# A searched order for a one-core decoder trunk: new orders for both plans, with the first output product inside the attention

## The chip, the cores and the metric

The kernel runs on one core of one Trainium2 chip. The metric is the device time of one execution in microseconds (us). Engines are named as in the profile: PE is TensorE (matmuls, with PEld for its weight loads), DVE is VectorE, ACT is ScalarE, POOL is GpSimd, SP is the engine that issues the transfers (DMAs).

## The reference

One layer over 1024 tokens of width 1024, everything in float32:

```python
h = rms_norm(x, norm1_g)
q, k, v, glu_a, glu_b = split(h @ w_in)            # five parts of 512 columns
q, k = rms_norm per head of 64 (8 heads)
attn = stick_breaking_attention(q, k, v)           # strictly causal, 128-query blocks
c = glu_a * sigmoid(glu_b)
c = silu(layer_norm(causal_depthwise_conv(c, 31 taps)))
x = x + concat([attn, c]) @ w_out
h = rms_norm(x, norm2_g)
gate, val = split(h @ w_up)                        # 2 x 2816 columns
gate = silu(causal_depthwise_conv(gate, 3 taps))
x = x + (gate * val) @ w_down
```

Stick-breaking attention weighs a key s before the query t by sigmoid(z) of its own score times the product of (1 - sigmoid(z)) of all keys between the two.

## The kernel before

**Products.** Every float32 operand is split into a high part (a rounded copy, made by ScalarE or by VectorE) and a low part (the difference, made by VectorE or GpSimd). `mm3` (L387 to L390) makes one product of three matmuls: high by high, high by low, low by high. A 128x512 output takes three matmuls for each 128 rows of the inner dimension.

**Stages.** (1) Input projection, GLU and 31-tap convolution, up to about 225 us. (2) Attention by head and half of the queries, up to about 414 us: `score` makes z, `below` (L1341) the sigmoids nb, `scan` (L1355) the running products, `turned` (L1374) transposes the weights into `wT`, `high` and `low` (L1385, L1395) split them, `products` (L1402) multiplies by v into the bank `po`, and `copied` and `summed` (L1430, L1436) put the head's rows into `attn`. Between these lie the convolution half of the output projection (`op`), whose sum with x is stored as `x_part`. (3) The attention half of the output projection by token tile of 128 (`opa`, in the order 0, 4, 1, 5, 2, 6, 3, 7), the second norm and the transposes `h2T` (L1678), from which the blocks 11, 21, 22, T1 to T4 are made: the operands of a seven-product (Strassen-like) scheme. (4) For each of 22 column blocks f of the FFN, seven products of 12 matmuls (11, 12, S2, S3, S1, S4, 22), sums into `gv`, and the activation. (5) The down projection (`dn`, L2099), from about 891 us.

**What sets the order.** Stages 1 to 4's beginning are written as two plans. Every piece of work is an operation made by `add(cost, emit, key, after, takes)`. Operations are numbered in the order in which they are defined. `ORDERS` holds one list of numbers for each plan, found by a search ahead of time; `plan.run` walks through the list, picks the engine where two are possible, gives out buffer slots and emits the instructions. `in_order` then chains the instructions of PE, DVE, ACT and POOL, each engine's in the order of the list. Transfers on SP are not chained, nor is the first plan with the second. Outside the plans the framework's scheduler places the instructions, and may move them between those of a plan.

**The first plan** ends with the last head (h = 7). The weights of the attention half of the output projection are loaded and split by `w_attn_rows` (L1547, L1551, L1556). **The second plan** begins with tile 0: its x is loaded back (L1623), the attention's rows of the tile are split into m (L1628 to L1638), two half products of 12 matmuls follow (`opa`, L388 to L390), and VectorE adds them to x (L1652). Its last part, `first_operands`, makes the operands and all seven products of FFN block 0, and the products 11 and 12 of block 1.

**Behind the second plan** stands the loop over f. For f = 0 the function `up` has no products left to make; it emits, in this order, y (ACT, L1948), two convolution steps (DVE, L1950), silu (ACT, L1952), the product with v (DVE, L1953) and a store. Then `sums_up(1)` emits the operands of block 1: three sums on POOL (L1769 to L1771), and for S2, S1, S3, S4 and 22 a cast on ACT (L384) and a subtraction on DVE (L385), with one more POOL sum (L1775) before S4. Products of block 1 other than 11 and 12 need those operands. The gate weights of block 2 are loaded into the buffer `raw0`, which holds those of block 1 until its operands are made.

Of the kernel before, what the change touches and what calls it, by code (L numbers as in the profile page):

```python
# [270 lines left out]
def kernel(  # L271
# [191 lines left out]
    def part_of(big_tile, i, words):  # L463
        return big_tile[:, i * words:(i + 1) * words]

    def in_order(start_at):
        last = {}
        for ins in nc.cur_bb.bb.instructions[start_at:]:
            if ins.engine in ORDERED:
# [1053 lines left out]
    for k in range(4):  # L1523
        w_out_rows(k)
# [615 lines left out]
```

## Time and profile before

| | |
|---|---|
| time, median of 3 runs | 1104.14 us (1103.88 to 1104.84) |
| the profiled execution's own time | 1106.51 us |
| its span | 1104.6 us |
| mean granted TensorE clock | 0.995 |
| matmuls, weight loads | 5258 each |
| DMA | 118.02 MB, mean 107 GB/s |

A row of a view by stretches gives, for each engine, its busy time in that stretch and in brackets the instructions that began there; PEclk is the clock that was granted to TensorE, as a share of full speed. A matmul of 128x512 is shown with some 0.39 us, but the next one starts 0.23 us after it: the matmuls overlap, so "busy" tells that TensorE had work, and the count of matmuls tells how much. A row of the waits gives the waiting instruction, what it waited for, the total, the times and the longest. A row of the timeline gives start, duration, engine, line, operation and tiles, and in square brackets the idle time ahead of it with what ended it.

### The profile page before, as it was taken

To read this page: it belongs to the slowest core of one execution; us is meant where nothing else is said; L and a number is where in the kernel's file an instruction comes from. 1 tells how busy PE (TensorE), PEld (TensorE's weight loads), DVE (VectorE), ACT (ScalarE), POOL (GpSimd) and SP (SyncE) were. 2 spreads that over 40 slices of the span, in tenths; PEclk is the share of its full clock that TensorE was granted. 3 is DMA by queue.
4 is the path that set the end of the run, shared out by engine and by line. 5 is a ranking of instruction groups with operands and counts; after the bars stand their busy time and mean duration, and the time that the engine had idled before them with its cause. 6 is when DMAs were issued, how large, how long until landed. Compare 5 with 4: busy or idle time off the path is not lost.

```text
span 1104.6 us, 14843 instructions
## 1 busy us (share of the span) xinstructions
PE 1091.2 (99%) x5258; PEld 908.6 (82%) x5258; DVE 882.3 (80%) x1201; ACT 586.5 (53%) x1044; POOL 591.0 (53%) x501
## 2 busy tenths in 40 slices
PE   8999999999999999999999999999999999999998
PEld 5888888888898887878888888888888888888887
DVE  6588998789999985889977777677777578797885
ACT  6354367576766663745333333343433388676760
POOL 4367889786722432894433223313322289887770
PEclk9999999999999999999999999999999999999999
DMA  8121210353843223523232222222231572403403
GB/s 271 39 58 39 86 49 20 86 177 105 260 119 95 96 91 139 188 80 96 96 107 65 96 77 82 90 77 96 71 102 58 175 301 77 152 22 132 153 5 149
DMA packets 110505, 118.02 MB, mean 107 GB/s; under 512 B 21369, under 2 KB 90208, under 8 KB 110430
## 3 DMA queue, kind: packets, MB, share of 16 engines
q1 hardware_dynamic: 110414, 117.06, 32.4%
q8 instruction: 42, 0.69, 0.3%
q14 instruction: 33, 0.27, 0.1%
q10 hardware_dynamic: 16, 0.00, 0.0%
HBM read 82.43 MB, written 28.31 MB: 100 GB/s over the span
## 4 chain that ended last, share of the span: by engine, by line
PE 96%; DVE 2%; ACT 1%; DMA 1%; issue 0%; SPq 0%; POOL 0%; DVEq 0%; POOLq 0%
PE dn L2099 19%; PE u_S L388 7%; PE u_S L389 7%; PE u_S L390 7%; PE u L390 5%; PE u L388 5%; PE u L389 5%; PE po L1402 3%; PE wT L1374 3%; PE qk L388 3%; PE qk L390 3%; PE qk L389 3%; PE z L1333 2%; PE z L1334 1%; PE opa L388 1%; PE opa L390 1%
## 5 line engine op out<-in xcount | busy, mean ns | idle before, releaser
L2099 PE MATMUL dn<-wd,wd 128*128 128x512 f32 x768 | 181.4, 389 | 0.0
L2099 PEld LDWEIGHTS dn<-wd,wd 128*128 128x128 f32 x768 | 144.2, 188 | 29.9
L388 PE MATMUL u_S<-bT,aS 128*128 128x512 f32 x264 | 102.7, 389 | 0.0
L389 PE MATMUL u_S<-bT,aS 128*128 128x512 f32 x264 | 102.7, 389 | 0.0
L390 PE MATMUL u_S<-bT,aS 128*128 128x512 f32 x264 | 102.6, 389 | 0.0
L2102 DVE TENSOR_TENSOR c<-dn,c 128x512 f32<-128x512 f32 x120 | 81.2, 686 | 24.9 <-PE dn L2099 24.6
L2004 ACT CAST wd<-rawd 128x512 fp32r<-128x512 f32 x128 | 72.8, 620 | 33.2 <-DMA rawd<-in_w_down_dram 10.0
L384 ACT CAST aS<-rawu 128x512 fp32r<-128x512 f32 x63 | 39.2, 624 | 94.6 <-PE u_S L390 66.1
L1355 DVE TENSOR_TENSOR_SCAN nb<-nb,one 128x384 f32<-128x384 f32 (+7 forms) x64 | 85.0, 1341 | 1.1 <-ACT nb L1341 0.9
L1769 POOL TENSOR_TENSOR s<-rawu 128x512 f32<-128x512 f32 x21 | 28.9, 1376 | 97.0 <-DMA rawu<-in_w_up_dram 95.6
L2003 ACT COPY whole<-rawd 128x512 f32<-128x512 f32 x110 | 63.5, 586 | 24.2 <-DVE wd L2005 11.4
L2005 DVE TENSOR_TENSOR wd<-whole,wd 128x512 fp32r<-128x512 f32 x90 | 59.9, 685 | 15.6 <-ACT wd L2004 8.5
L1775 POOL TENSOR_TENSOR rawu<-rawu 128x512 f32<-128x512 f32 x21 | 29.3, 1395 | 80.0 <-DVE a L385 79.9
L390 PE MATMUL u<-b,a 128*128 128x512 f32 x168 | 66.0, 393 | 2.0 <-DVE a L1903 2.0
L388 PE MATMUL u<-b,a 128*128 128x512 f32 x168 | 66.3, 394 | 0.0
L389 PE MATMUL u<-b,a 128*128 128x512 f32 x168 | 66.0, 393 | 0.0
L384 ACT CAST a<-rawu 128x512 fp32r<-128x512 f32 x61 | 37.9, 624 | 51.8 <-PE u_S L390 34.3
L1950 DVE SCALAR_TENSOR_TENSOR y<-gv,cols_a,y 128x1023 f32<-128x1023 f32 (+1 forms) x44 | 57.7, 1312 | 9.6 <-ACT y L1948 9.5
L1771 POOL TENSOR_TENSOR rawu<-s,rawu 128x512 f32<-128x512 f32 x21 | 31.7, 1508 | 49.6 <-DVE a L385 48.9
L389 PEld LDWEIGHTS u_S<-bT,aS 128*128 128x128 f32 x264 | 49.6, 188 | 10.3
L388 PEld LDWEIGHTS u_S<-bT,aS 128*128 128x128 f32 x264 | 49.6, 188 | 10.3
L390 PEld LDWEIGHTS u_S<-bT,aS 128*128 128x128 f32 x264 | 49.6, 188 | 10.3
(377 smaller groups left out, 3244.2 us busy)
## 6 DMA issues: line engine op xcount, KB each, us to landing
rawu<-in_w_up_dram SPq DMA_DIRECT2D x44, 512.0 KB
act_d<-y SPq DMA_DIRECT2D x22, 512.0 KB
rawd<-act_d SPq DMA_DIRECT2D x22, 512.0 KB
rawd<-in_w_down_dram SPq DMA_DIRECT2D x22, 512.0 KB
raw_qk<-in_w_in_dram SPq DMA_DIRECT2D x16, 256.0 KB
rawo<-in_w_out_dram SPq DMA_DIRECT2D x8, 512.0 KB
m<-conv_d SPq DMA_DIRECT2D x16, 256.0 KB
xt<-in_x_dram SPq DMA_DIRECT2D x8, 512.0 KB
```

The lines of the kernel that those rows point to most:

```text
L384: nc.scalar.copy(hi, src)
L388: nc.tensor.matmul(ps, a_hi, b_hi, start=first, stop=False)
L389: nc.tensor.matmul(ps, a_hi, b_lo, start=False, stop=False)
L390: nc.tensor.matmul(ps, a_lo, b_hi, start=False, stop=last)
L1355: nc.vector.tensor_tensor_scan(rev, rev, ones_of[0][:, :w], 0.0, op0=ALU.mult, op1=ALU.max)
L1374: nc.tensor.transpose(pt[:, 1 - j if diag else j, u * P:(u + 1) * P], ws[u][1]["nb"][:, ws[u][3] + sb * P:ws[u][3] + (sb + 1) * P], ident)
L1950: nc.vector.scalar_tensor_tensor(y[:, j:], g[:, :S - j], par("fw", (KF - 1 - j) * NF + f), y[:, j:], op0=ALU.mult, op1=ALU.add)
L2003: nc.scalar.copy(whole, src)
L2004: nc.scalar.copy(t[:, 0], src)
L2005: lo_engine.tensor_tensor(t[:, 1], whole, f32(t[:, 0]), op=ALU.subtract)
L2099: nc.tensor.matmul(ps, a[:, tok], b, start=first and m == 0, stop=last and m == 2, skip_group_check=True)
L2102: nc.vector.tensor_tensor(sums[c][s], ps, sums[c][s], op=ALU.add)
```

## The change

1. Both lists of `ORDERS` are replaced.
2. Costs in some operations are changed, and with them the engine that `plan.run` may pick. The normalising of x and the splitting of the `w_in` weights of v and qk are now marked `DVE2`, by which the planner reckons with DVE and POOL standing in each other's way.
3. The output product of tile 0 becomes 15 operations at the end of the first plan (`first_tile`), with m and x in the buffers raw0 and raw1 and its banks from those of the attention; the second plan has 8 operations fewer. The emitted instructions are the same in number and kind. Three dummy operations stand for the way from the last sums to the next tile.
4. The load of FFN block 0's first weights (into raw1) waits until tile 0's x has been used.
5. After the loop's first pass (f = 0) the instructions that it emitted on DVE, ACT and POOL are chained behind the second plan's last, in the order in which they were emitted. PE is left out of that chain.

By the new list the last operations of PE in the first plan are: `po` group 3 part 1, the first half product of tile 0 (1876 to 1879), `po` group 3 parts 2 and 3 (1720, 1724), the second half product (1881 to 1884). At the start, three transposes (tile 0's first half, both of tile 1) stand ahead of the first product of v; before it were tile 0's two. In the second plan PE's last eleven operations are 11 of block 0, two transposes of tile 7, 12 of block 0, 12 and 11 of block 1, and S3, S1, S2, 22, S4 of block 0.

```diff
 ORDERS = [[int(n) for n in numbers.split()] for numbers in ("""
...
+1870 1716 1876 1877 1722 1718 1723 1878 1879 1719 1720 1880 1724 1881 1882 1725
...
-    def in_order(start_at):
-        last = {}
+    def in_order(start_at, last=None, engines=ORDERED):
+        last = {} if last is None else last
         for ins in nc.cur_bb.bb.instructions[start_at:]:
-            if ins.engine in ORDERED:
+            if ins.engine in engines:
                 if ins.engine in last:
                     tc.add_manual_dep(ins, last[ins.engine].name, mybir.DependencyInfo(
                         mybir.DependencyClass.NoSync, mybir.DependencyReason.DATA), reason="planned order")
                 last[ins.engine] = ins
+        return last
...
-            c = add({"DVE": 560, "ACT": 650}, lambda eng, i=i, cols=cols: (
+            c = add({"DVE2": 520, "ACT": 830}, lambda eng, i=i, cols=cols: (
...
-            a = add({"ACT": 1330, "DVE": 1120}, high, T(at_ - LEAD_W), [x, begun_at], d["rooms"])
+            a = add({"ACT": 1440, "DVE2": 960}, high, T(at_ - LEAD_W), [x, begun_at], d["rooms"])
...
+    def first_tile(t, key):
+        d = tile_0
...
+        xl = add("SP", 4000, load, key - 2, [stored[t]], [xr])
+        a = add("ACT", 250, m_high, key, halves_done[0], [mr])
+        b = [add({"DVE2": 260, "POOL": 460}, low(3, lambda: attn[1][:, tok]), key, [a])]
+        a = add("ACT", 480, lambda: nc.scalar.copy(d["m"][:, 0, :3], attn[0][:, :, tok]), key, [a])
+        b += [add({"DVE2": 560, "POOL": 1000}, low(slice(0, 3), lambda: attn[0][:, :, tok]), key, [a])]
+        adds = []
+        for nn in range(2):
...
+                m = add("PE", 681, products, key + 0.1, b + last_unit + ([m] if m else []), [] if kk else [o])
+            f = add("DVE", 690, lambda nn=nn, cols=cols: nc.vector.tensor_tensor(d["x"][:, cols], d["ps", nn], d["x"][:, cols], op=ALU.add), key + 0.1, [m, xl])
...
+    first_tile(TOKENS[0], base - 0.4)
+    waits = add("DVE", 560, lambda: None, base, [add("ACT", 480, lambda: None, base, [halves_done[1][-1]])])
+    add("PE", 20, lambda: None, base + 0.5, [waits])
 
     plan.run(ORDERS[0])
     in_order(start_at)
...
-        a = add("ACT", 250, m_high, mk, [], [mr])
+        a = add("ACT", 250, m_high, mk, [last_sums] if t > 3 else [], [mr])
...
-        x1 = add("SP", 4500, lambda: load(0), key - 3)
+        x1 = add("SP", 4500, lambda: load(0), key - 3, tile_0["room"].users)
...
     plan.run(ORDERS[1])
-    in_order(start_at)
+    last_planned = in_order(start_at)
+    start_at = len(nc.cur_bb.bb.instructions)
...
         if f + 1 < NF:
             A = sums_up(f + 1, raw_next)
+        if f == 0:
+            in_order(start_at, last_planned, ORDERED[1:])
```

More of the change, by code (lines that the diff above doesn't have):

```diff
@@ L514, in load_x @@
         op = add("SP", 3500, load, key)
-        if not t:
-            op.moves = [Plan.HALF] * 2
+        if t < 2:
+            op.moves = [(360, 1500, 1750)] if t else [Plan.HALF] * 2
         return op
@@ L533, in roots @@
             nc.gpsimd.tensor_tensor(d["rs"], d["rs"], expo[:, :1], op=ALU.pow)
-        a = add("ACT", 1070 if t else 800, square, T(at_), [x], [r])
+        a = add("ACT", 1250 if t else 820, square, T(at_), [x], [r])
         b = add("POOL", 950, roots, T(at_), [a])
@@ L618, in weights @@
         x = add("SP", 3500, load, T(at_ - LEAD_LOAD) if key is None else key, [], [room])
-        x.moves = [Plan.PIECE] * 2 if len(srcs) > 1 else [Plan.COLUMNS]
+        x.moves = [(430, 2200, 1250 if name == "v_0" else 800), Plan.PIECE] if len(srcs) > 1 else [Plan.COLUMNS]
         if shape[0] < ND:
-            a = add({"ACT": 1330, "DVE": 1120}, high, T(at_ - LEAD_W), [x, begun_at], d["rooms"])
+            a = add({"ACT": 1440, "DVE2": 960}, high, T(at_ - LEAD_W), [x, begun_at], d["rooms"])
             b = add({"DVE2": 1480, "POOL": 3700}, low, T(at_ - LEAD_W + 0.5), [a])
@@ L1270, in unit @@
         return kst, k_ready, vst, v2
+    halves_done = [[], []]
     for h, half in [(h, half) for h in range(H) for half in range(2)]:
@@ L1440 @@
                 po.users += [a, b]
+                halves_done[half].append(b)
             prev_last = last
@@ L1519, in conv_half @@
                 xr.users += [f]
-            st = add("SP", 4000, lambda t=t, d=d: nc.sync.dma_start(x_part[t], d["x"]), k(1.2), sums)
+            st = stored[t] = add("SP", 4000, lambda t=t, d=d: nc.sync.dma_start(x_part[t], d["x"]), k(1.2), sums)
             xr.users += [st]
+    stored = {}
     for k in range(4):
@@ L1568, with load, m_high, low @@
     prev_last.after += last_unit
+    tile_0 = {}
+    def first_tile(t, key):
+        d = tile_0
+        tok = slice(t * P, (t + 1) * P)
+        mr, xr = [plan.token("wt", free=True) for _ in range(2)]
+        mr.only, xr.only = (0,), (1,)
+        def load():
+            d["x"] = raw([P, D], F32, f"x2_{t}", 1)
+            nc.sync.dma_start(d["x"], x_part[t])
+        def m_high():
+            d["m"] = raw([P, 2, 4, P], F32R, f"m{t}", 0)
+            nc.scalar.copy(d["m"][:, 0, 3], attn[1][:, tok])
+        def low(part, src):
+            return lambda eng: (nc.vector if eng == "DVE" else nc.gpsimd).tensor_tensor(d["m"][:, 1, part], src(), f32(d["m"][:, 0, part]), op=ALU.subtract)
+        xl = add("SP", 4000, load, key - 2, [stored[t]], [xr])
[5 more added lines that the diff above has]
+        for nn in range(2):
+            o, m = plan.token("o"), None
+            cols = slice(nn * 512, (nn + 1) * 512)
+            for kk in range(4):
+                def products(nn=nn, kk=kk, cols=cols, o=o):
+                    if kk == 0:
+                        d["ps", nn] = bank(o, [P, 512], f"opa{t}_{nn}")
+                    mm3(d["ps", nn], d["m"][:, 0, kk, :], d["m"][:, 1, kk, :], w_attn[ROWS[kk]][0][:, cols], w_attn[ROWS[kk]][1][:, cols], kk == 0, kk == 3)
+                m = add("PE", 681, products, key + 0.1, b + last_unit + ([m] if m else []), [] if kk else [o])
+            f = add("DVE", 690, lambda nn=nn, cols=cols: nc.vector.tensor_tensor(d["x"][:, cols], d["ps", nn], d["x"][:, cols], op=ALU.add), key + 0.1, [m, xl])
+            mr.users += [m]
+            o.users += [f]
+            adds.append(f)
+        mr.users += b
+        xr.users += adds
+    first_tile(TOKENS[0], base - 0.4)
+    waits = add("DVE", 560, lambda: None, base, [add("ACT", 480, lambda: None, base, [halves_done[1][-1]])])
+    add("PE", 20, lambda: None, base + 0.5, [waits])
     plan.run(ORDERS[0])
@@ L1612, with opa @@
     raws, block_done = {}, {}
-    def tokens(t, key):
-        hr, r = [plan.token(name) for name in ("h2", "small")]
-        xr, mr = plan.token("xt"), plan.token("m")
-        d = {}
-        tok = slice(t * P, (t + 1) * P)
-        where = (slice(None), slice(None), slice(t % 4 * P, (t % 4 + 1) * P))
+    def opa(t, key, d, tok, xr, adds):
+        mr = plan.token("m")
+        if t == TOKENS[1]:
+            mr.only = (1,)
         def load():
@@ L1631, in tokens @@
         xl.moves = [(360, 1500, 1800)]
-        adds = []
         mk = key + M_AT
-        a = add("ACT", 250, m_high, mk, [], [mr])
+        a = add("ACT", 250, m_high, mk, [last_sums] if t > 3 else [], [mr])
         b = [add({"DVE2": 260, "POOL": 460}, lambda eng: (nc.vector if eng == "DVE" else nc.gpsimd).tensor_tensor(
@@ L1655, in tokens @@
             adds.append(f)
+    def tokens(t, key):
+        hr, r = [plan.token(name) for name in ("h2", "small")]
+        d = {}
+        tok = slice(t * P, (t + 1) * P)
+        where = (slice(None), slice(None), slice(t % 4 * P, (t % 4 + 1) * P))
+        if t == TOKENS[0]:
+            d.update(tile_0)
+            xr, adds = Plan.Token("raw"), [add("DVE", 10, lambda: None, key, [attention_ends])]
+            tile_0["room"] = xr
+        else:
+            xr, adds = plan.token("xt"), []
+            opa(t, key, d, tok, xr, adds)
         st = add("SP", 3000, lambda: nc.sync.dma_start(x2_d[t], d["x"]), key, adds)
```

161 rows, old and new, of the table ORDERS are left out of this document.

## The prediction

> **What bounds the kernel now.** I read the page's busy times first, then stretches of the span side by side, then the waits of TensorE.
>
> ```profile
> span 1104.6 us, 14843 instructions
> PE 1091.2 (99%) x5258; PEld 908.6 (82%) x5258; DVE 882.3 (80%) x1201; ACT 586.5 (53%) x1044; POOL 591.0 (53%) x501
> ```
> ```profile
> core 0: us, PE busy (x) PEld busy (x) DVE busy (x) ACT busy (x) POOL busy (x), PEclk, DMA share, GB/s
> 7.00:14.00 7.00, 3.32 (x20) 2.12 (x19) 5.09 (x6) 6.04 (x11) 4.75 (x5) 1.00 1.06 377
> 14.00:19.00 5.00, 5.00 (x15) 3.93 (x16) 5.00 (x9) 3.84 (x7) 1.98 (x4) 0.66 1.04 403
> 50.00:225.00 175.00, 175.00 (x795) 144.39 (x794) 147.45 (x213) 93.93 (x180) 135.03 (x125) 1.00 0.20 58
> 225.00:406.00 181.00, 180.38 (x1177) 159.28 (x1176) 167.49 (x221) 124.67 (x248) 91.01 (x79) 1.00 0.43 129
> 406.00:415.00 9.00, 7.00 (x52) 6.00 (x51) 7.74 (x12) 6.71 (x13) 4.29 (x4) 0.99 0.79 255
> 415.00:419.00 4.00, 3.97 (x11) 3.11 (x12) 1.19 (x3) 0.39 (x1) 0.09 (x1) 0.61 0.56 221
> 466.00:479.20 13.20, 10.98 (x55) 8.47 (x53) 13.06 (x16) 9.90 (x19) 11.89 (x11) 1.00 0.39 121
> 479.20:483.00 3.80, 3.71 (x9) 2.95 (x10) 3.80 (x8) 1.74 (x3) 2.46 (x3) 0.55 0.15 45
> 483.00:500.00 17.00, 17.00 (x76) 13.96 (x75) 13.94 (x15) 6.64 (x11) 16.52 (x11) 1.00 0.29 83
> 500.00:1080.00 580.00, 580.00 (x2561) 480.41 (x2560) 447.72 (x602) 287.95 (x468) 281.10 (x209) 1.00 0.30 102
> ```
> ```profile
> PE v L739 <- DVE hi_v L598: 3.7, 2, 1.9
> PE u L390 <- DVE a L1903: 2.0, 1, 2.0
> PE opa L388 <- ACT m L1637: 1.4, 1, 1.4
> ```
> TensorE is the bound: 99% busy. From 500 to 1080 us it starts 2561 matmuls in 580 us, 0.2265 us for each 128x512 product, with no gap. So only four places can give anything. Each of the three great waits (DVE hi_v, ACT m, DVE a) is followed by a stretch with a granted clock of 0.66, 0.61 or 0.55, where busy TensorE starts fewer matmuls than the time has room for. A wait here is paid twice: as idle time and as slow clock.
>
> **The change part by part.** No instruction is added to or taken from any engine; the dummy operations of the new plan emit nothing. All is order.
>
> (a) *Tile 0's output product.* Counting the operations of the first plan in their order of definition, 1876 to 1879 and 1881 to 1884 are the two half products (12 matmuls each). The new list puts the first half ahead of the last head's last two `po` groups (1720, 1724) and the second half behind them.
>
> ```profile
> 412.53 0.38 PE L1402 MATMUL po<-tl,rest 128*128 128x256 f32 x1 [0.34 <-DVE tl L1395]
> 412.99 0.63 PE L1402 MATMUL po<-diagonal,rest 128*128 128x256 f32 x4
> 413.66 0.58 ACT L1430 COPY attn<-po 64x512 f32<-64x512 f32 x1 [0.96 <-PE po L1402]
> 414.27 0.89 DVE L1436 SCALAR_TENSOR_TENSOR attn<-po,v_ends,attn 64x256 f32<-64x256 f32 x2 [0.26 <-ACT attn L1430]
> 414.47 0.93 ACT L1637 CAST m<-attn 128x384 fp32r<-128x384 f32 x2
> 415.03 0.80 PE L388 MATMUL opa<-hio,m 128*128 128x512 f32 x1 [1.41 <-ACT m L1637]
> ```
> Lost here now: 9.00 - 7.00 = 2.0 us idle, and behind it 4.00 - 11 x 0.2265 = 1.5 us of slow clock; 3.5 in all. What is late next is tile 4, the first that needs the attention's end: copy 0.58, sums 0.89, half of the 0.93 cast, and three hand-overs of about 0.04, some 2.1 us behind the last `po`. The second half product takes 12 x 0.2265 = 2.7 us and covers it; without it the 1.4 us wait is back. The first half covers the wait on `tl`. Tile 0's load of x and its casts are moved past each other and past two weight loads on SP; they are 0.3 to 0.5 us pieces on engines with room (ACT 6.71 of 9 us). Value -3.5. Bounds: -3.5, and +1 if the last row of `w_out` is late and the product waits instead.
>
> (b) *The end of the second plan.* Lost now: 13.20 - 10.98 = 2.2 us idle and 3.80 - 9 x 0.2265 - 0.1 = 1.7 us of clock; 3.9.
>
> ```profile
> 475.79 1.77 DVE L1825 TENSOR_TENSOR a<-rawu,a 128x512 fp32r<-128x512 f32 x1
> 477.09 1.60 POOL L1832 TENSOR_TENSOR rawu<-rawu 128x512 f32<-128x512 f32 x1
> 477.49 1.75 DVE L1903 TENSOR_TENSOR a<-rawu,a 128x512 fp32r<-128x512 f32 x1
> 511.74 0.68 DVE L385 TENSOR_TENSOR aS<-rawu,aS 128x512 fp32r<-128x512 f32 x1
> ```
> VectorE is busy 13.06 of 13.20 us, and the same subtraction that takes 0.68 with GpSimd idle takes 1.75 beside a GpSimd tensor operation. The new order moves subtractions of tiles 4 and 5 (operations 49, 54, 56 and 111 of the old count) further ahead, into the time when both engines have room, so fewer collide at the end. A shift of the whole stage by (a) alone would leave this wait as it is, for the engines' inputs come at TensorE's pace. Bounds -3.9 and +2 (one more such collision of 1.1 us, and its clock). I take -3.3, nearest to the full removal, since 2 us of wait need only two of the 1.1 us collisions gone.
>
> (c) *The start.* Lost now: 7.00 - 3.32 = 3.7 us and 5.00 - 15 x 0.2265 = 1.6 us; 5.3.
>
> ```profile
> 9.54 0.80 PE L739 MATMUL v<-hi_v,h_hi 128*128 128x512 f32 x2 [1.82 <-DVE hi_v L598]
> 13.87 0.96 PE L739 MATMUL v<-hi_v,h_hi 128*128 128x512 f32 x3 [1.86 <-DVE hi_v L598]
> 10.37 3.44 DVE L598 TENSOR_SCALAR hi_v<-raw_v,gain 128x512 fp32r<-128x512 f32 x2
> 11.12 2.41 POOL L608 TENSOR_TENSOR lo_v<-raw_v,hi_v 128x1024 fp32r<-128x1024 f32 x1
> ```
> The second pair of `hi_v` took 3.44 us where the first two took 0.88, beside GpSimd's 2.41. The new order splits the second tile's work ahead of it and puts three turns of x in front of the first product: the second wait goes, the first grows, as tile 1 is normalised only after 10 us. Bounds -3.7 (first wait and half of the clock) and +1.5; I take -1.5, since TensorE is then in steady flow about 1 us sooner and part of the slow clock goes.
>
> (d) *The rest of the first plan.* From 50 to 225 us TensorE has no idle time, from 225 to 406 us 181.00 - 180.38 = 0.6, and small waits hidden in modelled ends. Bounds -2 and +2; I take -0.8.
>
> (e) *The wait that is added.* After the first FFN column block the change chains VectorE, ScalarE and GpSimd in the order of the code. There `up(0)` (the depthwise convolution, silu and product of block 0) stands ahead of `sums_up(1)` (the operands of block 1). In the trace they ran the other way:
>
> ```profile
> 488.93 0.62 ACT L384 CAST aS<-rawu 128x512 fp32r<-128x512 f32 x1 [2.77 <-POOL rawu L1770]
> 498.37 0.68 DVE L1868 TENSOR_TENSOR gv<-u_S,gv 128x512 f32<-128x512 f32 x1
> 499.08 1.25 ACT L1948 ACTIVATE y<-gv,cols_a 128x1024 f32<-128x1024 f32 x1 [0.53 <-DVE gv L1868]
> 500.36 2.60 DVE L1950 SCALAR_TENSOR_TENSOR y<-gv,cols_a,y 128x1023 f32<-128x1023 f32 x2 [0.21 <-ACT y L1948]
> 505.54 1.28 ACT L1952 ACT_TABLE_LOAD   x1
> 506.84 1.07 ACT L1952 ACTIVATE y<-y 128x1024 f32<-128x1024 f32 x1
> 510.10 1.72 DVE L1953 TENSOR_TENSOR y<-gv,y 128x1024 f32<-128x1024 f32 x1
> ```
> The cast at 488.93 for block 1 ran 10 us ahead of block 0's y. Chained, it queues behind y and silu on ScalarE, and its subtraction behind two convolution steps and the product on VectorE. TensorE is who waits: y needs block 0's last product (S4), block 1's products 11 and 12 are already used up, all others need these operands, and block 2's first weights go into the slot that block 1's operands are made from. From the last matmul of S4: its 0.39 us end, sum 0.68, y 1.25, steps 2.60, silu 1.07, product some 1.3 (1.72 beside GpSimd), subtraction 0.68, hand-overs 0.15: 8.1 us to the first matmul with a low part, less three slots of 0.2265: 7.4 us. A slow clock follows, as behind each wait above (1.5 to 1.7): 1.4. Bounds: 0, if the operands still come in time, and 12 with the 1.28 table load in the path and two slow stretches; nothing of it can be a gain, for TensorE has no gap from 483 to 500. I take +8.8.
>
> Sum: -3.5 - 3.3 - 1.5 - 0.8 + 8.8 = -0.3 us. It is made against the profiled span of 1104.6 (that execution's own time is 1106.51, 1.9 more); the median of the runs shown, 1104.14, is 2.4 below that execution, and I carry the difference over: **1103.8 us**.
>
> [...]
>
> **The rivals.** 0.2% (2.2 us) is about what a measurement of this kernel can tell from no change.
> - *The chain costs nothing*: the operands of block 1 are made in cover. For it: that chain concerns 18 instructions only; against it: the second plan's chain, made in the same way, was kept on VectorE where a later instruction was ready:
>
> ```profile
> 483.47 0.59 ACT L1875 COPY gv<-u 128x512 f32<-128x512 f32 x1 [1.86 <-PE u L390]
> 489.00 0.69 DVE L1868 TENSOR_TENSOR gv<-u_S,gv 128x512 f32<-128x512 f32 x1 [1.25 <-PE u_S L390]
> 489.61 0.68 DVE L1868 TENSOR_TENSOR gv<-u,gv 128x512 f32<-128x512 f32 x1
> ```
> The sum at 489.61 had its inputs at 484.1, and VectorE sat idle 1.25 us for the one ahead of it. Sum -9.1: 1095.0. Chance 0.15.
> - *The order gives more*: the start gives 4.5, the second plan's end 3.9, the middle 1.5. For it: all of that is idle time in the rows above; against it: the first product cannot start before `hi_v`, at 9.54. -3.5 - 3.9 - 4.5 - 1.5 + 8.8 = -4.6: 1099.5. Chance 0.25.
> - *Slower: VectorE stays the bound at the second plan's end.* The wait at 477 us is not recovered, since VectorE there has 0.14 us of room in 13.2: -0.3 + 3.3 = +3.0: 1107.1. It decides from 2.5 of the 3.3 us lost again; with the table load in (e)'s path 1108.4. Chance 0.22.
> - *Short waits cost no clock*: then (a) gives 2.0, (b) 1.7, (c) 1.1, (d) 0.8, and (e) stays at 8.8: +3.2, 1107.3. The clocks of 0.61 and 0.55 behind the two waits speak against it. Chance 0.02. [...]
>
> **How the numbers follow.** The forecast (no change that can be told) has 0.36, and 1102 to 1106.3 as its own range. Faster by over 0.2%: 0.15 + 0.25 = 0.40; slower: 0.22 + 0.02 = 0.24. Two cases of opposite sign (the price of the chain and the gains of the order) nearly cancel, so the range must hold both rivals: 1095 (chain free) to 1109 (its table load in the path, VectorE still the bound), with less than 2 in 10 outside.
>
> **What would show each step.** (a) no wait of `opa` on ACT `m`, and clock 1.00 in the 5 us behind the attention; (b) no wait of `u` on DVE `a`; (c) one wait on `hi_v` in place of two; (e) a wait of 6 to 8 us of `u_S` on a VectorE or ScalarE instruction of `sums_up(1)`, about 15 us behind the second plan's last `h2T`, with y at L1948's place ahead of all casts of block 1, and a slow clock behind it. The prediction is wrong if (e) shows no gap (then about 1095), or if a new wait stands between 50 and 406 us, where I saw hardly any room.

## The result

The changed kernel takes **1115.52 us** (median; 1114.90 to 1116.06) against 1104.49 us before (the three runs of the table of before and one more): ratio 1.0099, 95% interval 1.0081 to 1.0116. It is 11 us slower. The forecast was 1103.8 us, with a range that ended at 1109.

The page of the changed kernel begins so (its profiled execution took 1115.21 us, span 1112.9):

```profile
span 1112.9 us, 14818 instructions
PE 1088.1 (98%) x5258; PEld 905.4 (81%) x5258; DVE 871.7 (78%) x1200; ACT 586.9 (53%) x1050; POOL 580.6 (52%) x496
```

The work is the same: 5258 matmuls, and 2746 instructions on VectorE, ScalarE and GpSimd together in both. But ScalarE runs 6 more, VectorE 1 and GpSimd 5 fewer: by the new costs some changed their engine, so the change is not order alone, though the prediction says so. The span is 8.3 us longer. Where, is read from equal stretches of both spans. Before:

```profile
core 0: us, PE busy (x) PEld busy (x) DVE busy (x) ACT busy (x) POOL busy (x), PEclk, DMA share, GB/s
0.00:25.00 25.00, 20.19 (x81) 13.12 (x82) 14.15 (x28) 16.67 (x31) 10.21 (x22) 0.93 0.88 298
25.00:400.00 375.00, 374.38 (x2068) 319.38 (x2067) 325.66 (x448) 228.33 (x446) 232.65 (x209) 1.00 0.31 92
400.00:425.00 25.00, 22.97 (x123) 19.18 (x121) 17.50 (x24) 12.50 (x23) 8.95 (x8) 0.93 0.43 147
...
475.00:525.00 50.00, 48.02 (x204) 38.94 (x203) 45.67 (x49) 24.11 (x38) 32.46 (x23) 0.97 0.26 78
525.00:1080.00 555.00, 555.00 (x2450) 459.69 (x2450) 423.99 (x577) 275.33 (x449) 271.66 (x203) 1.00 0.30 102
```

After:

```profile
0.00:25.00 25.00, 21.43 (x94) 13.74 (x94) 14.21 (x31) 18.99 (x35) 6.83 (x21) 1.00 0.88 298
25.00:400.00 375.00, 370.27 (x2046) 315.74 (x2047) 314.40 (x438) 227.23 (x445) 236.81 (x211) 1.00 0.31 93
400.00:425.00 25.00, 22.99 (x129) 19.29 (x128) 19.87 (x28) 12.24 (x25) 7.09 (x7) 1.00 0.36 128
...
475.00:525.00 50.00, 39.57 (x166) 31.72 (x166) 38.69 (x45) 20.20 (x32) 26.28 (x18) 0.90 0.22 64
525.00:1080.00 555.00, 555.00 (x2450) 459.73 (x2449) 425.98 (x577) 276.78 (x453) 272.48 (x203) 1.00 0.30 102
```

Read the count of matmuls behind "PE busy". From 475 to 525 us all have the same shape: 166 in place of 204, and 38 x 0.2265 = 8.6 us. From 525 us on both kernels run 2450 in 555 us; nothing differs. At the start and at the attention's end the count is higher and the clock is 1.00 in place of 0.93, but in the middle (25 to 400 us) PE has 4.7 us without work where it had 0.6.

In the sections below "lost" is this: for each two neighbouring matmuls the time from start to start, less the step that undisturbed matmuls of those shapes take (0.2265 us for 128x512), added up over a stretch of the trace. It holds idle time and slow clock together. How the undisturbed step is chosen moves the row from 25 to 400 us by several us, but in all columns alike: the differences between the columns move by some 0.3 us.

| stretch, us | before | after | after without the chain |
|---|---|---|---|
| 0 to 25 | 9.45 | 7.89 | 8.01 |
| 25 to 400 | 16.55 | 19.33 | 19.34 |
| 400 to 425 | 5.07 | 3.49 | 3.44 |
| 425 to 475 | 2.06 | 1.73 | 1.64 |
| 475 to 525 | 4.29 | 12.83 | 1.69 |

TensorE's waits, after (what waited, for what, total us, times, longest):

```profile
PE u_S L387 <- ACT aS L383: 10.4, 1, 10.4
PE v L739 <- DVE lo_v L604: 1.9, 1, 1.9
PE qT L1290 <- DVE diagonal L1391: 1.7, 1, 1.7
...
PE wT L1375 <- DVE tl L1396: 1.2, 1, 1.2
PE glu_a L387 <- ACT cpad L827: 1.1, 1, 1.1
...
PE opa L387 <- ACT m L1683: 0.8, 1, 0.8
```

Of the three great waits of before, those on `hi_v` and on `a` are gone and that on `m` is 0.8 us in place of 1.4. In their place stand one of 10.4 us and a handful of 1 to 2 us. The long one in order of time (start, duration, engine, line, what, and in brackets the idle time before it with its releaser):

```profile
492.51 0.39 PE L389 MATMUL u_S<-b,aS 128*128 128x512 f32 x1
...
492.81 1.26 POOL L1829 TENSOR_TENSOR s<-rawu 128x512 f32<-128x512 f32 x1 [1.30 <-DMA rawu<-in_w_up_dram]
...
494.10 0.62 ACT L383 CAST aS<-s 128x512 fp32r<-128x512 f32 x1 [9.96 <-POOL s L1829]
494.75 1.08 DVE L384 TENSOR_TENSOR aS<-s,aS 128x512 fp32r<-128x512 f32 x1 [4.51 <-ACT aS L383]
495.76 0.68 DVE L1928 TENSOR_TENSOR gv<-u_S,gv 128x512 f32<-128x512 f32 x1
...
496.47 1.24 ACT L2009 ACTIVATE y<-gv,cols_a 128x1024 f32<-128x1024 f32 x1 [1.75 <-DVE gv L1928]
497.74 2.60 DVE L2011 SCALAR_TENSOR_TENSOR y<-gv,cols_a,y 128x1023 f32<-128x1023 f32 x2 [0.71 <-ACT y L2009]
500.42 1.28 ACT L2013 ACT_TABLE_LOAD   x1 [2.71 <-DVE y L2011]
501.72 1.06 ACT L2013 ACTIVATE y<-y 128x1024 f32<-128x1024 f32 x1
...
502.68 0.60 ACT L383 CAST aS<-rawu 128x512 fp32r<-128x512 f32 x1
...
503.33 0.79 PE L387 MATMUL u_S<-bT,aS 128*128 128x512 f32 x1 [10.43 <-ACT aS L383]
```

The reader is to see two things. From 495.76 on it is the forecast's path: last sum, y, two steps, silu, then the first cast of block 1, one after another on two engines. But the last sum's input was ready at 492.9, and it starts 2.9 us later, because VectorE holds another instruction: the subtraction at 494.75. It needs the cast at 494.10, and that the sum `s` at 492.81, for which GpSimd had waited for a transfer (`rawu`). Block 1's own `s` had been made at 487.46, so this is an operand of block **2**. Number 4 below, which holds back block 2's operands, takes it away.

### The profile page after: what moved, and what is told of

Read it like the earlier page. It is cut to its first block, busy times and chain, and to the rows that moved or that the text cites. A ratio compares the mean times of both kernels' runs of the same rounds, so it can differ in the third digit from the quotient of the medians.

```text
span 1112.9 us, 14818 instructions
## 1 busy us (share of the span) xinstructions
PE 1088.1 (98%) x5258; PEld 905.4 (81%) x5258; DVE 871.7 (78%) x1200; ACT 586.9 (53%) x1050; POOL 580.6 (52%) x496
## 4 chain that ended last, share of the span: by engine, by line
PE 86%; POOL 4%; DVE 3%; DMA 3%; ACT 2%; issue 2%; SPq 0%; DVEq 0%; POOLq 0%; ACTq 0%
PE dn L2162 19%; PE u_S L387 7%; PE u_S L388 7%; PE u_S L389 7%; PE u L387 5%; PE u L389 5%; PE u L388 5%; PE po L1403 3%; PE wT L1375 3%; PE qk L387 3%; PE qk L389 3%; PE qk L388 3%; POOL attn L879 2%; PE z L1334 2%; PE z L1335 1%
## 5 line engine op out<-in xcount | busy, mean ns | idle before, releaser
L387 PE MATMUL u_S<-bT,aS 128*128 128x512 f32 x264 | 103.9, 393 | 10.4 <-ACT aS L383 10.4
L1356 DVE TENSOR_TENSOR_SCAN nb<-nb,one 128x128 f32<-128x128 f32 (+7 forms) x64 | 84.6, 1340 | 0.6 <-ACT nb L1342 0.5
L2011 DVE SCALAR_TENSOR_TENSOR y<-gv,cols_a,y 128x1023 f32<-128x1023 f32 (+1 forms) x44 | 58.3, 1326 | 10.5 <-ACT y L2009 10.4
L389 PEld LDWEIGHTS u_S<-bT,aS 128*128 128x128 f32 x264 | 49.7, 188 | 10.4
L384 DVE TENSOR_TENSOR a<-rawu,a 128x512 fp32r<-128x512 f32 x61 | 45.4, 746 | 16.0 <-ACT a L383 16.0
```

Of the source, the lines that this page charges most:

```text
L384: lo_engine.tensor_tensor(lo, src, f32(hi), op=ALU.subtract)
L387: nc.tensor.matmul(ps, a_hi, b_hi, start=first, stop=False)
L389: nc.tensor.matmul(ps, a_lo, b_hi, start=False, stop=last)
L1356: nc.vector.tensor_tensor_scan(rev, rev, ones_of[0][:, :w], 0.0, op0=ALU.mult, op1=ALU.max)
L2011: nc.vector.scalar_tensor_tensor(y[:, j:], g[:, :S - j], par("fw", (KF - 1 - j) * NF + f), y[:, j:], op0=ALU.mult, op1=ALU.add)
```

## The experiments

Every kernel but the second starts from the changed one. Times are medians; the kernel before took 1104.92, 1105.07 and 1104.36 us beside the three sets.

**1. The chain left out** (both new orders stay).

```
         if f + 1 < NF:
             A = sums_up(f + 1, raw_next)
-        if f == 0:
-            in_order(start_at, last_planned, ORDERED[1:])
```

> The changed kernel without the chain behind the first FFN column block; both new orders stay. Theory (the chain carries the loss): the 10.4 us wait of u_S on aS and the slow clock behind it (2.3 us above the 0.2265 us step) are gone, nothing else moves: 1115.5 - 12.7 = 1102.8 us, so within 2 us of the kernel before, and the cast of block 1's S1 is ahead of y on ScalarE again. Rival 1 (the new orders lose time of their own, behind 475 us too): a wait of 3 us or more stays at 480 to 510 us and the time is 1106 or more. Rival 2 (the stall comes from the weights' transfers, and the chain only lies beside it): 1113 or more.

Measured 1103.13 us (1102.25 to 1103.84), ratio to before 0.9986, interval 0.9977 to 0.9995. The chain costs 12.4 us (by the lost time from 475 to 525 us of the two traces 11.1); all else together gains 1.8 (by the interval 0.6 to 2.5). The waits that remain:

```profile
PE hT L556 <- DVE x_k L549: 3.1, 2, 2.7
PE qT L1290 <- DVE diagonal L1391: 1.7, 1, 1.7
...
PE glu_a L387 <- ACT cpad L827: 1.2, 1, 1.2
...
PE opa L387 <- ACT m L1683: 0.8, 1, 0.8
PE u_S L389 <- DVE aS L1885: 0.7, 1, 0.7
```

No wait for an operand of block 1 is left (L1885 is block 0's own); behind the start the others stand as they did with the chain.

**2. The chain alone, on the kernel before** (both orders old; the same two lines and the argument of `in_order` added there).

> The kernel before with the chain alone; both orders are the old ones. Theory (the chain stalls TensorE whatever the order): one wait of 9.5 to 11 us of u_S on aS behind the second plan, about 2 us of slow clock, 1104.5 + 12 = 1116.5 us. Rival 1 (the chain hurts only in the new second order): a wait below 5 us, 1108 or less. Rival 2 (the forecast's size, 7.4 us of wait and 1.4 of clock): 1113.3.

Measured 1116.11 us, ratio 1.0109 (1.0095 to 1.0122). The chain does not need the new orders to do its harm. The wait itself was 7.6 us, not 9.5 to 11 as I expected: here the subtraction of block 2 was through (495.45 us) before block 0's last sum was due (496.88).

```profile
PE u_S L388 <- ACT aS L384: 7.6, 1, 7.6
```

TensorE lost 14.9 us from 475 to 525 us in place of 4.3. Of the 10.6 us more, 7.6 are the wait; the other 3.0 fit the slow clock behind it (21 products in 7.6 us at a granted clock of 0.63, which is 2.8 us more than they need).

**3. The chain kept, block 1's operands written ahead of `up(0)`.**

```
+        if f == 0:
+            A_1 = sums_up(1, raw_next)
         up(f, A)
         if f + 1 < NF:
-            A = sums_up(f + 1, raw_next)
+            A = sums_up(f + 1, raw_next) if f else A_1
```

> The changed kernel with block 1's operands written ahead of block 0's convolution in the code, so that the chain, kept, has them in that order. Theory (what stalls is the place of y, the table load and silu ahead of block 1's casts): the casts run before 490 us; the subtractions still stand behind block 2's first one (which waits for its weights to about 495) and two sums, so a wait of 3 to 5 us stays: 1115.5 - 7 = 1108.5 us. Rival (any chain across the two pieces stalls, because it stops the engines from running ahead): a wait of 8 us or more, 1113 or more. Rival 2 (operands first is as good as no chain): below 1104.

Measured 1105.51 us, ratio 1.0012 (1.0002 to 1.0021). So 10.0 of the chain's 12.4 us come from the place of block 0's vector work (y, the two steps, the table load, silu) ahead of block 1's operands, and not from a chain across the seam as such. Which of that work weighs most, this run doesn't tell. 2.4 us more than without the chain (number 1) stay. I expected 3 us more: TensorE had high parts to go on with while the subtractions came, and its longest wait there was 1.3 us.

```profile
PE u_S L387 <- ACT aS L383: 1.3, 1, 1.3
```

**4. Block 2's operands chained too,** so that they cannot stand ahead of block 0's sums.

```
+        if f == 1:
+            start_at = len(nc.cur_bb.bb.instructions)
         if f + 1 < NF:
             A = sums_up(f + 1, raw_next)
-        if f == 0:
+        if f < 2:
             in_order(start_at, last_planned, ORDERED[1:])
```

> The changed kernel with block 2's operand instructions put behind the chain as well, so that its first subtraction, which waits for its weights, no longer stands on VectorE ahead of block 0's last two sums. Theory (that subtraction adds 2.8 us to the forecast's path): the last sum starts within 0.3 us of the last product's end, the wait of u_S falls from 10.4 to 7.5 to 8 us, the time to 1112.7 us. Rival (block 2's weights or the slots set the stall): the wait stays above 10 us and the time at 1115 to 1116.

Measured 1111.71 us (1111.67 to 1112.68), ratio 1.0072 (1.0059 to 1.0084): 3.8 us less than the changed kernel by the medians, 3.0 by the ratios. Its timeline:

```profile
491.96 0.39 PE L389 MATMUL u_S<-b,aS 128*128 128x512 f32 x1
...
492.38 0.69 DVE L1928 TENSOR_TENSOR gv<-u_S,gv 128x512 f32<-128x512 f32 x1 [2.70 <-PE u_S L389]
...
497.06 1.28 ACT L2013 ACT_TABLE_LOAD   x1 [2.71 <-DVE y L2011]
...
499.98 0.79 PE L387 MATMUL u_S<-bT,aS 128*128 128x512 f32 x1 [7.63 <-ACT aS L383]
```

The sum now follows the product at once, and the wait is 7.63 us. One subtraction in a queue, two blocks ahead of its use, was worth 2.8 us of wait.

**5. The gap filled with products of zeros** (chain kept).

```
         up(f, A)
+        if f == 0:
+            warm = psz.tile([P, 512], F32, tag="z", name="warm")
+            start_w = len(nc.cur_bb.bb.instructions)
+            for _ in range(40):
+                nc.tensor.matmul(warm, zero_b, zero_b[:, :1].to_broadcast([P, 512]), start=True, stop=True)
+            in_order(start_w, last_planned, ORDERED[:1])
```

> The changed kernel, chain kept, with 40 added products of zeros (40 x 0.2265 = 9.1 us, an idle bank, nothing reads it) behind block 0's last product, inside the 10.6 us in which TensorE waits. Theory (the slow clock behind the wait is a price of idle TensorE, beside the wait): the wait shrinks to about 1.4 us, the next product starts at the same moment, and the products behind it come in steps of 0.2265 us: 1115.5 - 2.3 = 1113.2 us. Rival (the clock falls for a reason other than idle TensorE, or the steps are slow because the operands come late): 1115 to 1116 us, steps of 0.43 us as before.

Measured 1113.06 us (1112.30 to 1114.10): 2.5 us less than the changed kernel, with 9 us more work on TensorE. Stretches of the changed kernel, the wait and what follows:

```profile
492.90:503.30 10.40, 0.00 (x1) 0.00 (x0) 5.35 (x6) 4.72 (x6) 2.39 (x2) 0.68 0.00 0
503.30:507.00 3.70, 3.67 (x8) 2.63 (x9) 3.70 (x5) 2.06 (x4) 1.66 (x1) 0.51 0.38 145
```

and with the gap filled:

```profile
492.00:501.00 9.00, 8.94 (x42) 4.04 (x42) 4.85 (x5) 2.68 (x3) 2.48 (x2) 1.00 0.00 0
501.00:508.00 7.00, 5.01 (x21) 3.49 (x20) 5.44 (x6) 4.11 (x7) 2.85 (x2) 1.00 0.19 75
```

The operand came as late as before (the next product starts at 503.09 in place of 503.33 us), but the granted clock behind it is 1.00 in place of 0.51. So the slow clock is a price of its own, paid for the idleness, on top of the wait. Its size is less sure. In these two traces the eight products behind the wait took 3.69 and 2.54 us, and the down projection begins 1.4 us earlier with the gap filled (at 898.24 in place of 899.63 us); the medians, which come from more executions, give 2.5. So it is between 1.2 and 2.5 us, and the 1.4 that I had carried over from waits of 2 us lies within.

**6 and 7. The first plan's old order put back, without the chain:** first all of it up to tile 0's load (with the old prices), then only its middle.

> No chain; the first plan's operations in the order and with the prices of the kernel before up to the place where tile 0's load of x begins (1620 of 1889), behind it the new order with tile 0's product; the second plan's order is the new one. Theory (the new first order moves waits into 50 to 400 us): the waits at 142 us (glu_a, 1.3 us) and at 304 us (qT, 1.9 us) are gone, what TensorE loses from 25 to 400 us falls from 19.3 to about 16.6 us, the two waits of 2.0 us on hi_v at the start are back (9.4 us lost up to 25 us in place of 8.0): 1103.1 - 2.7 + 1.4 = 1101.8 us. Rival (the two waits are the price of tile 0's early loads and stay): 1104.5 us or more, since the start is the old one.

> No chain; the first 150 operations and those behind the 1620th in the new order, between them the order of before, all with the new prices. Theory (the new first order gains at the start and loses in the middle): one wait on x_k at the start, none at 142 and at 304 us: 1103.1 - 2.7 = 1100.4 us. Rival (the waits in the middle follow from where the new start leaves the engines, or from the new prices that choose between ScalarE and VectorE): the waits stay, 1103 us.

Measured 1107.90 (ratio 1.0028, 1.0019 to 1.0037) and 1108.72 us (1.0035, 1.0023 to 1.0047): slower, against my theory. The waits at 142 and 304 us were gone, as expected, but both runs had one, at 362 us, that neither parent has:

```profile
PE kT L1255 <- POOL keys L1241: 3.9, 1, 3.9
```

GpSimd makes those keys, and the seam at the 1620th operation had put them behind an addition that waits for a product. From these two alone nothing could be said on the order.

**8. The same with the seam earlier,** at the 1371st operation (about 311 us), where both orders have done the same work but for five operations.

> As the run with the new start and the old middle, but the old order ends at the 1371st operation (about 311 us by the sum of TensorE's prices) in place of the 1620th; there the two orders have come equally far but for five operations, and GpSimd's and ScalarE's work for the last head's keys stands as in the new order. Theory (the wait of 3.9 us on keys at 362 us came from the join; the waits at 142 and 304 us belong to the new first order): none of the three, TensorE loses 13 to 14 us from 25 to 350 us in place of 15.7: 1103.1 - 2.3 = 1100.8 us. Rival (old middle and new end do not fit, wherever they are joined): a wait of 3 us or more behind 311 us, 1104 or more.

Measured **1101.61 us** (1100.80 to 1102.38), ratio 0.9977 (0.9968 to 0.9987), the fastest of all. None of the three waits is there:

```profile
PE v L739 <- DVE lo_v L604: 1.7, 1, 1.7
PE hT L556 <- DVE x_k L549: 1.4, 1, 1.4
...
PE kT L1255 <- DVE diagonal L1391: 1.0, 1, 1.0
```

The wait on `diagonal` is a new one (0.4 us before). TensorE lost 14.6 us from 25 to 350 us in place of 15.7, where I had expected 13 to 14 (13.2 before; 1.4 us more stay at 25 to 50 and 225 to 250 us together, from the new start or the new prices, which no run parts). So the searched order of the middle was worse than the old one, by 1.0 us (the ratios to before) to 1.5 us (the medians). The intervals of the two ratios overlap, but numbers 10 and 11 below differ by the same edit, ran beside each other, and lie 1.2 us apart.

**9. Tile 0's two half products behind the attention's last product** (chain out; operations 1876 to 1885 moved behind 1726).

> No chain; both new orders, but tile 0's two half products stand behind the last product of the attention in place of ahead of it and between; its casts stay where they are. Theory (the products only choose which wait they cover): the wait of 0.96 us on m of tile 4 is gone, as 5.4 us of products lie ahead of it; the last po groups lose the first half as cover and wait 0.5 to 1 us longer: 1103.1 us, within 0.7. Rival 1 (the move into the attention is what gained): 1104.5 to 1105. Rival 2 (the cover behind is worth more): 1102 or less.

Measured 1104.82 us (1103.80 to 1105.55), ratio 0.9999 (0.9991 to 1.0007): 1.4 us (by the ratios) to 1.7 us (by the medians) more than with the products inside, and 1.6 by the time lost from 400 to 425 us (5.07 against 3.44). The last `po` groups wait 0.6 and 0.7 us without that cover. And the wait of `opa` on `m` at 420 us is there all the same, 0.8 us, though 5.4 us of products stood ahead of it in place of 2.7: it cannot be the attention's end that it waits for. On ScalarE tile 1's cast, which is ahead of tile 4's, sat until tile 0's last matmul:

```profile
420.79 0.30 ACT L1675 CAST m<-attn_last 128x128 fp32r<-128x128 f32 x1 [4.56 <-PE opa L389]
```

**10 and 11. Tile 4's cast ahead of tile 1's** in the second plan (`21 52 23` becomes `21 23 52`), alone and with number 8. ScalarE in number 1, at that place:

```profile
418.52 0.30 ACT L1675 CAST m<-attn_last 128x128 fp32r<-128x128 f32 x1
420.76 0.30 ACT L1675 CAST m<-attn_last 128x128 fp32r<-128x128 f32 x1 [1.94 <-PE opa L389]
420.96 0.51 ACT L1683 CAST m<-attn 128x384 fp32r<-128x384 f32 x1
```

The second line is tile 1's cast. It takes the slot that tile 0's product still reads, and waits for its last matmul; tile 4's cast stands behind it in the queue. The second plan takes slot 0 of `m` as free at its start, since tile 0 now belongs to the first plan.

> No chain; both new orders, but in the second plan the cast of tile 4 (operation 23) stands ahead of tile 1's first cast (operation 52), which waits on ScalarE for the slot that tile 0's product still reads. Theory (the wait of 0.8 us of opa on m behind the attention is this queue, not the attention's end): that wait falls below 0.3 us, 1103.1 - 0.7 = 1102.4 us. Rival (tile 4's sums end too late anyway): the wait stays at 0.7 us or more, 1103.1 us.

> Both of the last two edits. Theory (they stand in different places and add up): 1103.1 - 2.3 - 0.7 = 1100.1 us, 0.4% below the kernel before. Rival (what one saves is given back at the next wait): 1102 or more.

Measured 1102.95 us (ratio 0.9990, 0.9980 to 1.0000) and 1101.77 us (0.9975, 0.9966 to 0.9984): no gain over numbers 1 and 8. The cast came at 420.23, but the wait only changed its name:

```profile
PE opa L389 <- DVE m L1684: 1.1, 1, 1.1
```

On VectorE tile 4's subtraction (the second line) stands behind the addition of x, which waits for tile 0's product in the same way:

```profile
421.94 0.69 DVE L1608 TENSOR_TENSOR x<-opa,x 128x512 f32<-128x512 f32 x1 [1.34 <-PE opa L389]
...
422.85 0.56 DVE L1684 TENSOR_TENSOR m<-attn,m 128x384 fp32r<-128x384 f32 x1
```

One queue was mended and the other not; with both mended it wasn't tried.

## Why the prediction was wrong, step by step

The forecast of 1103.8 us was 11.7 too low. 3.6 us of this lie in the chain (12.4 for 8.8) and 7.3 in the gains (1.8 for 9.1). The other 0.8 is the kernel before, whose median was 1104.14 us when I forecast, and 1104.49 and 1104.92 beside the changed kernel and number 1.

**(e), the chain: right in place and path, but the path lacked a member.** Forecast +8.8 (7.4 of wait, 1.4 of clock); measured 12.4 us of time (number 1 against the changed kernel). The path of 7.4 us was nearly right: 7.63 us in number 4, 7.6 in number 2, though its last members were others. The 1.28 us table load, which I had left to the upper bound, is in the path; the product and the subtraction, which I had in it, are not, since the first matmuls need the cast alone. What I missed is block 2's subtraction, 2.8 us of wait (number 4). I had asked what the chained instructions would stand behind, but not what unchained ones the compiler would now put ahead of them. The second term, 1.4 us of clock, can't be called wrong: number 5 gives 1.2 to 2.5. The wait began 22 us behind the second plan's last `h2T`, where I had said about 15.

**(d), the middle of the first plan: wrong sign, and at 3.6 us the largest single miss.** Forecast -0.8; the table shows +2.8, and number 8 shows the order to be the cause of 1.0 to 1.5 us of it. The cause of the rest stays open. I had seen "hardly any room" there and so taken a loss for unlikely; but an order that gains nothing can lose. My own sign ("wrong if a new wait stands between 50 and 406 us") names it.

**(a), tile 0's product: half.** Forecast -3.5; lost time from 400 to 425 us fell by 1.6, and number 9 gives the product's place 1.4 to 1.7 us. The wait on `m` fell from 1.4 to 0.8 us, but did not go, though I had announced that. Not the attention's end holds it but instructions ahead of tile 4's that wait for tile 0's product: number 9 shows this, number 10 that it is more than one queue. And a wait of 1.2 us of `wT` on `tl` at 409.9 us is new (0.3 before). It stands in every trace that has the new end of the first plan, number 9 included, so it belongs to that order and not to the place of the product.

**(b), the second plan's end, and (c), the start: right in the trace.** (b) forecast -3.3: without the chain the lost time from 425 to 525 us fell from 6.35 to 3.33, and the wait of `u` on `a` is gone. So is the collision that I had named. From 472 to 479 us, in the kernel before and in number 1 (columns as above):

```profile
472.00:479.00 7.00, 5.31 (x27) 3.90 (x25) 7.00 (x5) 3.96 (x8) 6.84 (x6) 1.00 0.26 76
472.00:479.00 7.00, 7.00 (x32) 5.47 (x31) 6.82 (x10) 4.29 (x8) 3.17 (x3) 1.00 0.26 76
```

GpSimd is busy 3.17 us in place of 6.84, and VectorE gets through 10 instructions in place of 5. (c) forecast -1.5: 9.45 to 7.89. The two waits on `hi_v` are gone, and one of `hT` on tile 1's `x_k` has come in their place (1.5 us; I had expected it on `hi_v`); a wait of 1.9 us on `lo_v` can follow just behind 25 us. One slip in the working: the bound of -3.7 is not the first wait and half of the clock (1.8 + 0.8 = 2.6), and the rival's 4.5 lies outside it.

**The gains together, and the baseline.** In the traces 3.3 us fewer are lost without the chain, where 9.1 were forecast. Of the 5.8 us that are missing, (d) is 3.6, (a) 1.9 and (b) 0.3. In the medians only 1.8 of the 3.3 us arrive, for the profiled execution of before lies 1.6 us above the median of its kind, and number 1's only 0.4. (a), (b) and (c) counted on up to 1.5, 1.7 and 1.6 us of slow clock, read from one execution. Beside the experiments the kernel before ran 68 more times, and its time goes with its mean granted clock: 1102.8 us at 1.000 (5 runs, median), 1103.5 at 0.998 (25), 1105.1 at 0.997 (25), 1105.8 at 0.995 (13). The profiled execution, 1106.51 us at 0.995, was slower than all but 4 of them. Three stretches of half clock of 3.41 us followed its three great waits. Each lowers the mean clock of such a span by 0.0015 (half of 3.41 of 1104), so by that working 0.995, 0.997 and 0.998 are three, two and one of them, and the typical run has fewer than three. I noted the 2.4 us between that execution and the median and carried them over, but the gains I then subtracted were partly the same microseconds.

Put together, from the table: -1.6 (c), +2.8 (d), -1.6 (a), -0.3 and +8.5 behind 425 us ((b) and (e) together), which is +7.8; the span grew by 8.3. The median grew by 11.0, since the execution shown of before had more half clock than most.

Of the rivals, "slower" came true, but not by its mechanism: VectorE did not stay the bound at the second plan's end. Only the table load, its further 1.3 us, was in the path. "The order gives more" and "the chain costs nothing" are refuted by numbers 1 and 2. Against "short waits cost no clock" stands before's own trace: at its waits of 1.4 and 2.0 us (up to 415.03 and 479.29 us) the granted clock fell to 0.50, from 414.73 to 418.15 and from 479.59 to 483.00 us. But its 68 runs, with mean clocks from 0.995 to 1.000, show that the price is paid in some executions and not in others. The changed kernel's trace has half clock once before the last product, for 10.24 us (496.68 to 506.92), from within the long wait on.

The length of a wait alone does not tell whether it is paid. In before's trace the wait of 1.8 us that ended at 9.54 us cost no clock (1.00 from 5.13 to 15.37 us), and neither did those of 1.5, 1.9 and 1.7 us that ended at 9.08, 26.08 and 306.38 us in the changed kernel's (1.00 from 5.16 to 496.68 us); the 1.4 us before `opa` did. What decides it, no run here shows.

## What to carry to other kernels

When a pinned piece meets a piece that the compiler orders by its own estimate, look at the compiled order of each engine on both sides of the seam: what counts is not only what the pin holds back but what the compiler then moves ahead of it, above all an instruction that waits for a transfer. Write the operands of the next block ahead of the long vector work of this one; here that alone turned +11 us into +0.6, though leaving the chain out was 2.4 us better still. And before pricing a slow clock, see from several executions how often it is paid.

## What the runs showed of the hardware

The price of a wait of TensorE has two parts that can be told apart: filling a 10 us gap with products of zeros took the half clock behind it away (1.00 in place of 0.51) and saved 2.5 us by the medians (1.4 in the two traces), though the operand came as late. Behind waits of 1.4 to 2 us the half clock comes in some executions only: the same program took 1102.18 to 1107.16 us, sorted by its mean granted clock from 1.000 to 0.995, and the changed kernel's own trace has waits of 1.9, 1.7 and 1.5 us with the clock at 1.00 from 5.2 to 496.7 us. Half clock was granted for 3.41 us at a time in before's trace, up to its last product, and for 10.24 us in and behind the changed kernel's wait of 10.4 us. Starts of the same order also differed: in the first 25 us the changed kernel was granted 1.00 and started 94 matmuls, number 1 was granted 0.93 and started 89.
